# The order of the instruction queues, chosen with another timing model, in a one-core transformer layer

## The chip, the cores and the metric

The kernel runs on one core of a Trainium2 chip. A core has five engines, each with its own queue of instructions, worked off in the order in which it was written at build time: TensorE (PE, with its weight loads, PEld), VectorE (DVE), ScalarE (ACT), GpSimd (POOL) and SyncE (SP), which here mostly starts transfers. Engines wait for each other by semaphores. The metric is the time of one execution on the device, in microseconds.

## The reference

One layer of a latent-diffusion backbone, in float32: 1024 latent tokens and 256 context tokens, width 1024. Cut to what matters:

```
mod   = silu(c) @ w_mod + b_mod                      # shifts, scales, gates of two norms
h, hc = modulated rms_norm of x and of ctx
proj  = h @ w_in                                     # q k v | mLSTM q k v o gates | branch gates
att   = windowed GQA: 16 heads in 4 groups, |i-j| <= 128, all 256 context keys, a sink logit per head
ml    = bidirectional chunkwise mLSTM, started from the context's states, normed, times sigmoid(o)
y     = sigmoid(ga) * (att @ w_branch_att) + sigmoid(gm) * (ml @ w_branch_ml)
x_mid = x + g1 * (y @ w_out)
u     = depthwise conv, width 3, of norm2(x_mid) @ w_up          # 2 x 2816 columns
out   = x_mid + g2 * ((silu(u_g) * u_a) @ w_down)
```

## The kernel before

Every float32 operand is split in a high part (rounded to the fast float32 format of PE) and a low rest: ACT copies the high part, DVE subtracts it (`split_from`, lines 44 and 49). Each product is three matmuls, high by high, high by low and low by high (`mm3`, lines 91 to 93).

The stages follow each other in the source and overlap at their ends. *Start* (to about 105 us): the modulation from sixteen loads `wm` of 512 KB, the norms, transposes of x (`xct`), the context's keys and values. *Attention* (about 105 to 655 us). *mLSTM* (to about 1050 us), with the projections `mo` between its chunk steps. *Branch products and out-projection* (to about 1300 us). *FFN*: 22 units of the up-projection, written as a seven-product scheme on 2x2 blocks (products `pa`, `pb`, `pc`; operand sums and their splits `t1`..`t4`, `b21`, `b22` on DVE and ACT). *Down-projection* in the same scheme (`dx`, `dy`, `finish`), to the end.

The attention's loop takes the 32 pairs (g, b), a group of four heads with one of eight blocks of 128 tokens, as a software pipeline:

```
    for n in range(N + 5):
        if n < N:
            proj(*seq[n])
        if 0 <= n - 1 < N:
            stacks(*seq[n - 1])
        if 0 <= n - 3 < N:
            scores(*seq[n - 3])
        if 0 <= n - 4 < N:
            pv(*seq[n - 4])
        if n not in SKIPS and n < N + len(SKIPS):
            filler(n - sum(s < n for s in SKIPS))
```

`proj` makes q, k and v of one block (24 matmuls into `pq`), with the norm's sums on ACT, DVE and POOL and the rotary products on DVE (lines 520 to 545). `stacks` turns q and k (PE `qt`, then ACT and DVE into `QT`, `KA`, `KB`, lines 553 to 570). `scores` makes for each of four heads the scores `s` (four matmuls, lines 587 to 590) in a PSUM pool with **one** buffer (`s_tile`); DVE adds the mask and takes the row's extreme into `P` (line 593), ACT takes the exponential (line 597), DVE and POOL divide by the sum (lines 601 to 606). `pv` turns `P` (line 625, tile `pt`), splits it (`ph` on ACT, `pl` on DVE) and multiplies with the values (lines 619 and 620, tile `po`); the result `o` leaves by line 636. `filler` is independent work: one half of a 128-column block of the branch gates' projection, 24 matmuls into `g`, 5 to 6 us of PE, whose weights (`fr`) are loaded and split (`fh`, `fl`) just ahead. A `mod_product` (line 212, `macc`) adds one 256 KB slab of the second modulation matrix, loaded into the single buffer `wmb`; lines 221 to 228 (`ms`, `gT`) finish a row of it. The branch weights' sums are lines 1047 to 1050 (`s_ba`).

**What sets the order.** The kernel is written without engine queues of its own. At build time the tile context takes all instructions and picks, in a simulated time, for each engine the next one to be put in its queue: of those whose inputs and buffers are ready in that simulation, the one that stands first in the source. So how long the planner thinks each instruction takes, and when it thinks a buffer comes free, decides which work from further down the source is drawn ahead of work that it believes not yet ready. In ten places `issue_after` holds work back until a named instruction has been put in its queue (for instance lines 309, 445, 909, 1228, 1439 and 1451). The buffers (PSUM: two `mm` for `pq` and `po`, three `tp` for `qt` and `pt`, one `fl` for `g`, the one `s`) turn in the order so found. The chip then keeps each queue's order, whatever its real times are.

## Time and profile before

| | before |
|---|---|
| median of 3 runs | 1943.81 us (1943.13 to 1944.04) |
| profiled execution, span from first to last instruction | 1937.4 us |
| PE busy | 1903.1 us (98%) |
| DVE, ACT, POOL busy | 1442.4, 1000.5, 332.0 us |
| mean granted clock of PE | 0.999 |
| moved by DMA | 298.53 MB, 154 GB/s on average |

The profile is of one execution. A *window* row gives a stretch of it: start and end, its length, the busy time of PE, PEld, DVE, ACT and POOL with their counts of instructions, the granted clock of PE (1.00 is full), and the DMA engines' share and rate. A *group* row gives source line, engine, operation, tile names with shapes and count, then busy time and the mean duration of one in ns, then the time for which the engine was idle just before such an instruction and what ended it. Busy times of neighbours overlap a little, since an engine starts the next instruction before the one in front has quite finished. A *timeline* row gives start and duration in us of one instruction, or of some alike.

### The profile page before, as it was taken

What the parts mean: (1) busy time and instruction counts of PE and PEld (TensorE: products, weight loads), DVE (VectorE), ACT (ScalarE), POOL (GpSimd) and SP (SyncE); (2) the same over time, 40 slices, a digit from 0 to 9 for tenths busy, and PEclk for the clock granted to TensorE, in tenths of its full rate; (3) what the DMA queues carried; (4) which work ended last, traced back from release to release, by engine and by line L of the source; (5) the groups of instructions that cost most, each with busy time, mean ns of one, the idle gap of its engine ahead of it and who ended that gap; (6) DMA issues with size and microseconds to landing.
All of it is one profiled execution on the core that took longest, in us unless ns stands there. A gap on an engine that the chain in (4) does not pass through costs nothing.

```text
span 1937.4 us, 28767 instructions
## 1 busy us (share of the span) xinstructions
PE 1903.1 (98%) x10012; PEld 1631.2 (84%) x10012; DVE 1442.4 (74%) x2886; ACT 1000.5 (52%) x1979; POOL 332.0 (17%) x534
## 2 busy tenths in 40 slices
PE   8999999999999999999999999999999999999999
PEld 3998888888888889999999888788888888888887
DVE  2867878777777666666657878669989898897564
ACT  4845656555556445353536556256545444455441
POOL 1323433433333132131311012010000000000000
PEclk9999999999999999999999999999999999999999
DMA  8731222313222323425235982722354534499841
GB/s 320 231 126 51 80 66 67 95 42 102 60 67 77 125 89 104 144 94 192 88 106 210 376 300 89 279 94 77 141 199 182 195 152 177 160 327 341 307 165 65
DMA packets 139377, 298.53 MB, mean 154 GB/s; under 512 B 15440, under 2 KB 39648, under 8 KB 136416
## 3 DMA queue, kind: packets, MB, share of 16 engines
q1 hardware_dynamic: 124832, 270.48, 40.3%
q10 hardware_dynamic: 14400, 26.22, 4.0%
q8 instruction: 78, 1.28, 0.3%
q14 instruction: 67, 0.55, 0.1%
HBM read 220.55 MB, written 76.10 MB: 153 GB/s over the span
## 4 chain that ended last, share of the span: by engine, by line
PE 83%; DVE 5%; DMA 4%; ACT 4%; issue 2%; POOL 1%; POOLq 0%; ACTq 0%; SPq 0%; DVEq 0%
PE pa L1513 4%; PE pa L1515 4%; PE pa L1514 4%; PE pt L625 3%; PE g L93 3%; PE g L92 3%; PE g L91 3%; PE yb L1515 2%; PE yb L1514 2%; PE yb L1513 2%; PE dx L1515 2%; PE dx L1513 2%; PE dx L1514 2%; PE pb L1513 2%; PE pb L1515 2%
## 5 line engine op out<-in xcount | busy, mean ns | idle before, releaser
L606 POOL TENSOR_SCALAR P<-P,st 128x640 f32<-128x640 f32 (+1 forms) x128 | 115.1, 916 | 261.0 <-DVE st L604 178.3
L597 ACT ACTIVATE P<-P,st 128x640 f32<-128x640 f32 (+1 forms) x128 | 102.6, 801 | 24.6 <-DVE st L593 24.0
L593 DVE CUSTOM_DVE_ANT_0 P<-s,maskA,nsink 128x640 f32<-128x640 f32 (+1 forms) x112 | 103.2, 921 | 9.4 <-PE s L590 7.8
L49 DVE TENSOR_TENSOR pl<-pt,ph 128x512 fp32r<-128x512 f32 x152 | 100.8, 686 | 10.1 <-ACT ph L44 8.6
L44 ACT ACTIVATE ph<-pt 128x512 fp32r<-128x512 f32 x152 | 87.4, 597 | 36.9 <-PE pt L625 32.5
L91 PE MATMUL g<-hH,fh 128*128 128x512 f32 x256 | 102.7, 401 | 0.0
L93 PE MATMUL g<-hH,fl 128*128 128x512 f32 x256 | 100.6, 393 | 0.0
L92 PE MATMUL g<-hL,fh 128*128 128x512 f32 x256 | 100.6, 393 | 0.0
L625 PE MATMUL pt<-ident,P 128*128 128x128 f32 x608 | 92.3, 273 | 3.5 <-POOL P L606 3.1
L91 PE MATMUL pq<-w1h,hH 128*128 128x384 f32 (+1 forms) x256 | 87.1, 340 | 0.2 <-DVE t L545 0.2
L91 PE MATMUL kv<-w1h,hH 128*128 128x384 f32 x256 | 86.5, 339 | 0.8 <-ACT w1h L44 0.8
L93 PE MATMUL pq<-w1h,hL 128*128 128x384 f32 (+1 forms) x256 | 86.7, 339 | 0.0
L92 PE MATMUL kv<-w1l,hH 128*128 128x384 f32 x256 | 86.6, 338 | 0.0
L92 PE MATMUL pq<-w1l,hH 128*128 128x384 f32 (+1 forms) x256 | 86.5, 338 | 0.0
L93 PE MATMUL kv<-w1h,hL 128*128 128x384 f32 x256 | 86.3, 337 | 0.0
L625 PEld LDWEIGHTS pt<-ident,P 128*128 128x128 f32 x608 | 71.1, 140 | 11.5 <-POOL P L606 6.4
L91 PE MATMUL mo<-w1h,hH 128*128 128x256 f32 x256 | 72.6, 284 | 0.4 <-ACT sg L774 0.2
L93 PE MATMUL mo<-w1h,hL 128*128 128x256 f32 x256 | 72.1, 282 | 0.0
L92 PE MATMUL mo<-w1l,hH 128*128 128x256 f32 x256 | 71.9, 281 | 0.0
L1651 ACT ACTIVATE cv<-ua,vecT 128x1024 f32<-128x1024 f32 x22 | 27.4, 1245 | 83.6 <-DVE ua L1624 83.6
L929 POOL TENSOR_SCALAR kwh<-k,gcall 128x128 fp32r<-128x128 f32 x72 | 32.7, 457 | 215.8 <-PE dC L92 112.1
L1513 PE MATMUL dx<-dwh,dfh 128*128 128x512 f32 x176 | 68.7, 390 | 0.0
(587 smaller groups left out, 6392.9 us busy)
## 6 DMA issues: line engine op xcount, KB each, us to landing
ur<-in_w_up SPq DMA_DIRECT2D x22, 1024.0 KB, 4.9
wmb<-in_w_modB SPq DMA_DIRECT2D x48, 256.0 KB, 2.9
f_d<-cv SPq DMA_DIRECT2D x22, 512.0 KB, 2.6
wm<-in_w_modA SPq DMA_DIRECT2D x16, 512.0 KB, 9.2
fr<-in_w_g SPq DMA_DIRECT2D x32, 256.0 KB, 3.1
drf<-fs_d SPq DMA_DIRECT2D x15, 512.0 KB, 6.8
drw<-wt_d SPq DMA_DIRECT2D x14, 512.0 KB, 6.0
w1b<-in_w_cx SPq DMA_DIRECT2D x16, 388.0 KB, 4.0
```

The costliest lines, as they stand in the source:

```text
L44: return nc.scalar.activation(out, in_, AF.Copy, scale=scale)
L49: (nc.vector if eng == "v" else nc.gpsimd).tensor_tensor(lo, src, hi.bitcast(F32), op=ALU.subtract)
L91: nc.tensor.matmul(ps, lh[:, ls], rh[:, rs], start=start and i == 0, stop=False)
L92: nc.tensor.matmul(ps, lh[:, ls], rl[:, rs], start=False, stop=False)
L93: nc.tensor.matmul(ps, ll[:, ls], rh[:, rs], start=False, stop=stop and i == n - 1)
L593: nc.vector.tensor_tensor_reduce(pm[:, :W], ps[:, off : off + W], mask[:, :W], scale=ss[:, h : h + 1], scalar=nsink[:, hh : hh + 1], op0=A ...
L597: nc.scalar.activation(pm[:, :W], pm[:, :W], AF.Exp, bias=st4[:, h : h + 1], scale=-1.0, accum_out=st4[:, 4 + h : 5 + h])
L606: nc.gpsimd.tensor_scalar(Ps[h][:, :W], Ps[h][:, :W], st4[:, 12 + h : 13 + h], 1.0, op0=ALU.mult, op1=ALU.mult)
L625: nc.tensor.transpose(pt[:, h * P : (h + 1) * P], Ps[h][:, kb * P : (kb + 1) * P], ident)
L1513: nc.tensor.matmul(ps, lh, rh, start=start and i == 0, stop=False, skip_group_check=True)
L1514: nc.tensor.matmul(ps, lh, rl, start=False, stop=False, skip_group_check=True)
L1515: nc.tensor.matmul(ps, ll, rh, start=False, stop=stop and i == n - 1, skip_group_check=True)
```

## The change

One argument is added where the tile context is made, in `kernel`, line 1927:

```diff
-    with tile.TileContext(nc) as tc:
+    with tile.TileContext(nc, schedule_with_timeline_sim=True) as tc:
         layer_kernel(tc, A, out)
```

The planner then works with the finer timing model that the language offers instead of its simple one. The operations, their shapes and operands, the pools and the pins are the same. What differs is the order in each engine's queue, and with it which buffer an instance gets and where waits stand: stand-alone waits are 144 instead of 127 on PE, 817 becomes 724 on ACT, 664 becomes 750 on DVE and 589 becomes 560 on SP. ACT has 14 activation table loads instead of 10.

The places where the order differs most:

```
attention      fillers g are put in the queue earlier, up to 12.9 us of them in one block; eleven of the 32
               blocks have none; none is left after the last block's scores. Branch-weight sums s_ba
               (lines 1047 to 1050) stand on DVE before the last scores instead of after them.
mLSTM          the products mo stand in smaller groups between the chunk steps
FFN's start    pa1 and pc1 stand on PE ahead of the transposes x2p1; on DVE t3l, b22l, q2l, t4l stand ahead of t2l
FFN's units    the first products of the next unit (pb t1, pa b11) stand earlier
down-proj.     the last two rows of the modulation (ms, gT, the gate's row) stand some 20 us of PE work later;
               30 matmuls of dy_3 stand in one lump
start          SP: masks, sink, gate bias, first attention weights and first wmb ahead of wm_4 and the later wm;
               POOL: the rotary tables earlier; DVE: seven macc sums earlier
```

## The prediction

> **What bounds the kernel now.** I read the busy shares first, then the slices, then the chain that ended last, and then windows over each stage.
>
> ```profile
> span 1937.4 us, 28767 instructions
> PE 1903.1 (98%) x10012; PEld 1631.2 (84%) x10012; DVE 1442.4 (74%) x2886; ACT 1000.5 (52%) x1979; POOL 332.0 (17%) x534
> ...
> DVE  2867878777777666666657878669989898897564
> ...
> PE 83%; DVE 5%; DMA 4%; ACT 4%; issue 2%; POOL 1%; POOLq 0%; ACTq 0%; SPq 0%; DVEq 0%
> ```
>
> PE is idle for 1937.4 − 1903.1 = 34.3 us in all, so a better order can gain no more than that. The other engines keep up with PE, but DVE only just: nine tenths and more in several late slices. The windows (span, then busy time of PE, its weight loads, DVE, ACT and POOL, then granted clock, DMA share and GB/s) show where the slack is.
>
> ```profile
> 131.80:640.00 508.20, 499.09 (x2836) 437.63 (x2835) 385.36 (x962) 298.56 (x671) 181.36 (x239) 1.00 0.24 70
> ...
> 278.90:291.50 12.60, 12.28 (x74) 10.65 (x73) 11.03 (x28) 7.98 (x19) 2.41 (x4) 1.00 0.14 45
> 378.90:392.60 13.70, 13.13 (x84) 11.92 (x83) 11.41 (x31) 8.08 (x21) 4.99 (x9) 1.00 0.20 64
> ...
> 655.00:1050.00 395.00, 384.31 (x2538) 361.00 (x2536) 263.98 (x754) 181.51 (x458) 93.49 (x214) 1.00 0.37 125
> ...
> 1299.00:1316.00 17.00, 16.46 (x81) 13.36 (x80) 16.45 (x43) 12.93 (x35) 2.47 (x1) 1.00 0.20 62
> 1316.00:1330.00 14.00, 13.73 (x60) 10.83 (x59) 14.00 (x28) 10.37 (x22) 0.00 (x0) 1.00 0.22 76
> 1400.00:1500.00 100.00, 100.00 (x443) 82.81 (x442) 89.21 (x106) 46.94 (x58) 0.00 (x0) 1.00 0.52 192
> ...
> 1760.00:1850.00 90.00, 90.00 (x407) 74.70 (x406) 58.38 (x96) 40.59 (x71) 0.00 (x0) 1.00 0.86 309
> ```
>
> Attention (131.8 to 640) holds 9.1 us of PE's idle time, the mLSTM (655 to 1050) 10.7 us. At the FFN's entry (1299 to 1330) DVE is full too. In the steady FFN PE has no gap at all.
>
> **The change, part by part.** No instruction is dropped, but for four more activation table loads; what moves is the order in each engine's queue. So a cost can only be idle time of PE that the new order forces, and a gain only idle time that it fills. I take the work between two points from the trace of before, start to start, and set it against the new order.
>
> *Attention.* One block is one (g, b) of the 32: scores, softmax, transposes, values, plus projection of a later block. Before, each block also carries one filler, 24 `g` matmuls. The prices:
>
> ```profile
> L593 DVE CUSTOM_DVE_ANT_0 P<-s,maskA,nsink 128x640 f32<-128x640 f32 (+1 forms) x112 | 103.2, 921 | 9.4 <-PE s L590 7.8
> L49 DVE TENSOR_TENSOR pl<-pt,ph 128x512 fp32r<-128x512 f32 x143 | 94.9, 686 | 5.1 <-ACT ph L44 3.6
> L212 DVE SCALAR_TENSOR_TENSOR macc<-wmb,sil,macc 128x512 f32<-128x512 f32 x35 | 29.0, 829 | 21.4 <-DMA wmb<-in_w_modB 21.4
> L567 DVE TENSOR_TENSOR QT<-qt,QT 64x256 fp32r<-64x256 f32 x60 | 25.3, 422 | 6.5 <-ACT QT L44 5.1
> ...
> L636 DVE TENSOR_TENSOR o<-po,o 64x512 f32<-64x512 f32 x30 | 20.4, 681 | 5.9 <-ACT o L44 5.2
> L543 DVE TENSOR_TENSOR qf<-pq,TA 128x256 f32<-128x256 f32 (+1 forms) x58 | 18.3, 316 | 0.0
> L49 DVE TENSOR_TENSOR w1l<-w1r,w1h 128x768 fp32r<-128x768 f32 x17 | 17.4, 1031 | 1.7 <-ACT w1h L44 1.7
> ...
> L593 DVE CUSTOM_DVE_ANT_0 P<-s,mask,nsink 128x512 f32<-128x512 f32 x12 | 9.7, 807 | 1.4 <-PE s L590 1.3
> ```
>
> ```profile
> L1047 DVE TENSOR_TENSOR s_ba<-s_ba,s_ba 128x512 f32<-128x512 f32 x4 | 2.8, 693 | 6.7 <-DMA s_ba<-in_w_ba 6.7
> ```
>
> ```profile
> 308.46 0.42 PE L587 MATMUL s<-KA,QT 128*128 128x384 f32 x1
> ...
> 309.12 1.03 PE L625 MATMUL pt<-ident,P 128*128 128x128 f32 x8
> 309.91 0.48 PE L91 MATMUL g<-hH,fh 128*128 128x512 f32 x1
> ...
> 316.15 0.48 PE L619 MATMUL po<-ph,V 128*128 128x512 f32 x1
> ...
> 317.49 0.40 PE L93 MATMUL g<-hH,fl 128*128 128x512 f32 x1
> ...
> 319.01 0.40 PE L93 MATMUL g<-hH,fl 128*128 128x512 f32 x1
> ...
> 321.31 0.34 PE L91 MATMUL pq<-w1h,hH 128*128 128x384 f32 x1
> ...
> 325.53 0.38 PE L558 MATMUL qt<-ident,qf 128*128 128x128 f32 x2
> ```
>
> ```profile
> 131.80:640.00 508.20, 181.37 (x671) 123.61 (x672) 16.11 (x27) 1.00 0.24 70
> ```
>
> The last row is the same window for tile `g` alone. Start to start, PE needs 0.66 us for a head's scores, 0.79/8 = 0.10 for a `pt` transpose, 1.34/5 = 0.27 for a `po` matmul, 2.30/10 = 0.23 for a `g` matmul (24: 5.5 us) and 4.22 for a projection. The stretch has 112 + 12 = 124 heads on line 593, so 31 blocks: a block is 499.09/31 = 16.1 us of PE against 385.36/31 = 12.4 of DVE. It holds 28 fillers (671 `g` matmuls of 24 each), so a block with one has about 16.6 us of PE work and a block without one 11.1. So PE stays the bound only in a block with its filler. The new order draws fillers ahead: PE's work between the first scores of successive blocks becomes
>
> ```
> block  0    1    2    3    4    5    6    7    8    9   10   11 ... 17   18 ... 25   26   27   28   29   30
> us   17.8 22.6 18.1 14.9 24.6 24.8 17.7 11.9  3.5 17.7  3.9 19.1  10.5  8.2   16.1 11.5 10.5  8.9  6.1  6.7
> ```
>
> and eleven blocks have no `g` matmul left. Scores go through one PSUM buffer (`s_tile`): the scores of head k+1 wait until line 593 has read head k, and DVE does that in its queue's order. So between two heads PE cannot be quicker than DVE's queue. Adding, over disjoint stretches of heads, what DVE's work exceeds PE's: in the old order the sum is 0, in the new one 39 us. The stretches, with heads counted from 0:
>
> ```
> heads     12-15  32-36  37-42  45-51  71-74  76-81  107-110  112-126  smaller
> DVE        11.6    6.0   16.9   20.9    6.5   20.8     6.5     35.9
> PE          8.5    2.9   10.7   18.2    2.4   18.5     3.1     24.2
> excess      3.1    3.0    6.2    2.8    4.1    2.2     3.4     11.7     2.5
> ```
>
> The largest is followed by hand: 14 heads on line 593 at 0.92 (12.9), 15 `pl` at 0.69 (10.3), the branch-weight sums of lines 1047 to 1050, 8 at 0.69 (5.5), which the old order has after 660 us, 3 `o` (2.0), 2 `w1l` (2.1), 4 `QT` (1.7) and 3 to 4 us of small ones: 38 by means, 35.9 start to start, since neighbours overlap a little. PE has 13 heads of scores, 60 `pt` and 34 `po` matmuls there: 8.6 + 6.0 + 34 × 0.27 = 24. This is a bound from below as far as the order goes; it leaves out hand-overs between engines. At the end the last block's softmax has 22 `g` matmuls as cover before and none after: 22 × 0.23 = 5.1 us, from which I take 4. Against it, the new order may fill some of the 9.1 us of gaps; I take 1 for that. Attention: +39 + 4 − 1 = **+42**, from +25 (gaps all filled, overlap of DVE's work better by a tenth) to +65.
>
> The chip's clock adds something.
>
> ```profile
> 930.00:935.00 5.00, 2.91 (x19) 2.25 (x18) 5.00 (x9) 2.69 (x8) 5.00 (x8) 0.92 0.01 3
> 935.00:940.00 5.00, 5.00 (x33) 5.00 (x34) 4.05 (x18) 3.55 (x11) 1.20 (x4) 0.74 0.00 0
> ```
>
> ```profile
> 735.00:740.00 5.00, 3.13 (x25) 2.90 (x24) 4.76 (x15) 3.40 (x12) 5.00 (x9) 1.00 0.00 0
> ...
> 835.00:840.00 5.00, 3.43 (x25) 3.15 (x26) 4.99 (x16) 2.78 (x9) 4.36 (x14) 1.00 0.00 0
> ```
>
> PE busy for 2.91 of 5 us lost clock (0.92, then 0.74: 5 × 0.26 = 1.3 us of work lost); 3.13 and 3.43 of 5 did not. Of the stretches above two fall below that share, 32-36 (2.9 of 6.0) and 71-74 (2.4 of 6.5); most keep PE two thirds busy. **+2**, from 0 to 8 × 1.3 = 10. [...]
>
> *FFN entry.* In the new order `pa1` and `pc1` (5.5 us of PE) stand ahead of the transposes `x2p1`, and DVE has 15 us of work between `acc0<-fb0` and the last `t2l`, where the old order has 7.3 (`t3l`, `b22l`, `q2l` and `t4l` come ahead, 0.34 us each or 0.60, start to start); PE has 10.9 us there, ACT about 1 more in front. The rows of 1299 to 1330 show DVE without a gap, so nothing absorbs it: 15.1 − 10.9 + 0.9 = **+5** (0 to the 7.8 that DVE has more).
>
> *Steady FFN.* A unit is bound by PE (100.00 of 100, DVE 89.21); the new order starts the next unit's first products a little earlier: 0 (−1, to +4 if each of 22 units lost 0.2).
>
> *mLSTM.* Its gaps wait on DVE and POOL (735, 835 and 930); the new order spreads the `mo` products over them: **−3** (−8, most of the 10.7; to +3, one more gap like that at 930: 2.1 and 1.3 of clock).
>
> *Down-projection.* The last rows of `modB` and the gate's transpose come about 20 us later, close to where `finish` must free PSUM, in a window with a DMA share of 0.86, and `dy_3`'s 30 matmuls then stand in one lump: **+2** (0 to 30 × 0.23 = 7).
>
> *Start.* SP issues ten loads (masks, attention weights, the first `wmb`, some 1.95 MB) ahead of the later `wm`; POOL builds the rotary tables earlier.
>
> ```profile
> wm<-in_w_modA SPq DMA_DIRECT2D x16, 512.0 KB, 9.2
> ```
>
> ```profile
> 65.00:70.00 5.00, 2.94 (x20) 2.41 (x20) 4.72 (x6) 4.58 (x10) 5.00 (x6) 1.00 0.55 159
> ```
>
> At `wm`'s pace in the list of DMA issues (0.5 MB in 9.2 us with others beside it, mostly its own kind) 1.95 MB would at most delay a load by several us; `wm` loads are issued well ahead of their products, and PE's 2.1 us without work at 65 may go. **0** (−2 to +6).
>
> *Table loads.* Four more on ACT, which is busy for half the span:
>
> ```profile
> L1011 ACT ACT_TABLE_LOAD x3 | 3.8, 1283 | 0.1
> ```
>
> 4 × 1.28 = 5.1 us, hidden: 0 (to +3, where ACT is late for `ph`). The branch products and the out-projection keep their order: 0.
>
> Sum: 42 + 2 + 5 − 3 + 2 = +48. The profiled execution, 1937.4 us by its span, becomes 1985; the median of 1943.81 stands 6.4 above that span: 1943.81 + 48 = **1992 us**.
>
> **The rivals.** (a) *Faster.* If DVE runs ahead before a stretch without fillers, line 593 is never late, and only filled gaps count. For it: the windows at 278.9 and 378.9 cover blocks with few `g` matmuls, and PE still has 12.28 of 12.6 and 13.13 of 13.7 us. Against it: with one `s` buffer DVE cannot run ahead on scores, and those blocks stand alone. It decides where a block's DVE work fits PE's (11 us against 12, as in those windows). The gain would be the mLSTM's 8, the start's 2 and 5 of attention's 9.1: 1929 us. (b) *Only the end of attention and the FFN entry.* Short stretches are smoothed by neighbours, heads 112 to 126 are not: 12 + 4 + 5 − 3 = +18: 1962. (c) *A chain instead of a sum.* Without cover each block pays its hand-overs, scores to 593 to exponential to POOL to `pt` to `ph` to `po`, and DVE's queue is held by `macc` waiting for `wmb` (21.4 us of waits in the row above, now ahead of heads that PE needs), plus the clock: eleven blocks at 3 us beside the sum, +33: 2025. (d) *No change within what a measurement tells*, 0.2% or 4 us: it needs gain and loss to cancel; 1944.
>
> **How the numbers follow.** My forecast (1975 to 2010) 0.55, (b) 0.15, (c) 0.20, (d) 0.02, (a) 0.08. Range: (a) and (d) with half of the tail of (c) are left out: 1955 to 2030. Faster by over 0.2% 0.07, within 0.2% 0.02, slower 0.91. The three runs of before spread over 0.91 us, so 0.2% is what a measurement tells.
>
> **What would show it.** Right: PE's idle time grows by 40 us or more, nearly all between 200 and 700; idle rows of PE name DVE line 593 (`s` waiting) or `ph` and POOL in the stretches listed; the windows of blocks 7 to 10 and 26 to 31 show DVE near full and PE at two thirds; the FFN's entry shows 5 us more. Wrong: DVE also idle in those windows (a chain, (c)), or PE at 0.98 there (a); clock rows well under 1.00 in attention would make the clock's term bigger; and a longer wait of `pm` for `wm` the start's.

## The result and the profile after

The changed kernel takes 2059.45 us in the median of four runs (2057.10 to 2061.17), the kernel before 1943.47 in four (1941.81 to 1944.04). The ratio is 1.0604, with a 95% interval of 1.0586 to 1.0622: 116 us longer. The forecast was 1992 with a range up to 2030. The direction was right and the size was not; the time lies beyond the range.

The first lines of the profile's page, after:

```profile
span 2055.2 us, 28709 instructions
PE 1942.5 (95%) x10012; PEld 1663.7 (81%) x10012; DVE 1454.2 (71%) x2886; ACT 1004.5 (49%) x1983; POOL 322.4 (16%) x534
...
PE 76%; DVE 9%; DMA 7%; issue 3%; ACT 3%; POOL 1%; ACTq 0%; DVEq 0%; SPq 0%; POOLq 0%
```

PE executes the same 10,012 matmuls. It is idle for 2055.2 − 1942.5 = 112.7 us instead of 34.3 (78 more), and it is busy 39 us longer, because its mean granted clock is 0.976 instead of 0.999. In the chain that ended last, DVE's share has nearly doubled and that of transfers has risen by three points: PE now waits for others, and these wait for data.

The stages, as windows: attention from the first scores to the last `po`, the mLSTM to the last `mt`, and behind the last `op` the FFN's entry, its steady units and the rest to the end. First before, then after:

```profile
131.80:657.60 525.80, 516.65 (x2937) 452.21 (x2936) 395.39 (x983) 308.18 (x693) 185.85 (x252) 1.00 0.24 70
657.60:1050.70 393.10, 382.39 (x2530) 359.64 (x2529) 263.08 (x751) 181.60 (x458) 93.49 (x214) 1.00 0.37 125
...
1298.60:1330.00 31.40, 30.59 (x140) 24.51 (x140) 30.85 (x71) 23.71 (x56) 2.47 (x1) 1.00 0.21 68
1330.00:1721.40 391.40, 391.40 (x1726) 323.61 (x1725) 347.95 (x415) 195.85 (x243) 0.00 (x0) 1.00 0.48 178
1721.40:1937.40 216.00, 211.56 (x942) 175.01 (x940) 142.20 (x225) 82.94 (x145) 0.00 (x0) 1.00 0.65 231
```

```profile
130.80:730.10 599.30, 543.94 (x2954) 472.38 (x2952) 399.12 (x991) 305.71 (x692) 175.08 (x255) 0.97 0.22 68
730.10:1147.90 417.80, 389.96 (x2513) 370.61 (x2512) 270.52 (x744) 191.41 (x468) 93.70 (x211) 0.94 0.33 109
...
1395.00:1426.40 31.40, 26.98 (x113) 21.60 (x112) 27.52 (x68) 19.75 (x49) 3.01 (x1) 0.89 0.20 67
1426.40:1820.10 393.70, 384.09 (x1682) 314.44 (x1682) 332.39 (x395) 189.93 (x234) 0.00 (x0) 1.00 0.45 161
1820.10:2055.20 235.10, 228.24 (x1014) 188.47 (x1012) 161.21 (x253) 93.51 (x163) 0.00 (x0) 1.00 0.66 239
```

Attention lost 599.3 − 525.8 = 73.5 us, the mLSTM 24.7, and the FFN with its down-projection 660.2 − 638.8 = 21.4. The start (131.8 before, 130.8 after) and the branch and out-projections gained 1 us each. In attention PE is idle for 55.4 us instead of 9.1. The entry's window is cut to the same 31.4 us in both, but only 113 matmuls start in it after instead of 140, so the time that they lack appears in the later rows.

What PE waited for, as groups of waits after (us in total, times, longest):

```profile
PE s L587 <- DVE st L593: 27.1, 22, 2.7
PE pt L625 <- POOL P L606: 7.8, 20, 1.1
PE pa L1513 <- ACT ug L44: 6.9, 7, 1.0
PE po L619 <- ACT ph L44: 6.4, 9, 1.6
...
PE pa L1513 <- ACT ua L44: 5.2, 2, 2.7
```

Before, the first of these was `PE s L587 <- DVE st L593: 0.5, 1, 0.5`. So scores wait for line 593, as the forecast named it. But DVE is not simply full. Its own waits after, of which the first two were 9.1 and 8.6 us before, while that for `wmb` was 28.6 and has not grown:

```profile
DVE P L593 <- PE s L590: 67.8, 48, 3.9
...
DVE pl L49 <- ACT ph L44: 50.1, 45, 4.0
...
DVE macc L212 <- DMA wmb<-in_w_modB: 26.8, 20, 2.8
```

PE waits for DVE, and DVE waits for PE, ACT and transfers, in turn. That is the picture of a chain. The end of attention, six blocks without a filler, shows it in windows:

```profile
640.00:665.00 25.00, 19.62 (x106) 17.50 (x105) 18.20 (x49) 14.35 (x33) 11.03 (x16) 0.86 0.06 11
665.00:690.00 25.00, 19.60 (x111) 16.72 (x109) 20.84 (x50) 15.72 (x34) 8.72 (x12) 0.93 0.38 111
690.00:731.00 41.00, 33.67 (x174) 26.52 (x174) 30.13 (x64) 22.95 (x51) 12.89 (x31) 0.92 0.31 95
```

They take 91 us, 15.2 a block. DVE is busy for 69.2 of these, PE for 72.9 even at a clock of 0.86 to 0.93, and no other engine more. No engine is full, and yet a block costs 15 us.

### The profile page after: what moved, and what is told of

Read it like the earlier page. It is cut to its first block, busy times and chain, and to the rows that moved or that the text cites. A ratio compares the mean times of both kernels' runs of the same rounds, so it can differ in the third digit from the quotient of the medians.

```text
span 2055.2 us, 28709 instructions
## 1 busy us (share of the span) xinstructions
PE 1942.5 (95%) x10012; PEld 1663.7 (81%) x10012; DVE 1454.2 (71%) x2886; ACT 1004.5 (49%) x1983; POOL 322.4 (16%) x534
## 4 chain that ended last, share of the span: by engine, by line
PE 76%; DVE 9%; DMA 7%; issue 3%; ACT 3%; POOL 1%; ACTq 0%; DVEq 0%; SPq 0%; POOLq 0%
PE pa L1513 4%; PE pa L1514 4%; PE pa L1515 4%; PE pt L625 2%; PE g L91 2%; PE yb L1514 2%; PE yb L1515 2%; PE g L93 2%; PE g L92 2%; PE yb L1513 2%; DMA wmb<-in_w_modB 2%; PE pb L1514 2%; PE pb L1515 2%; PE pb L1513 2%; PE dx L1513 2%
## 5 line engine op out<-in xcount | busy, mean ns | idle before, releaser
L593 DVE CUSTOM_DVE_ANT_0 P<-s,maskA,nsink 128x640 f32<-128x640 f32 (+1 forms) x112 | 103.0, 920 | 62.4 <-PE s L590 61.3
L49 DVE TENSOR_TENSOR pl<-pt,ph 128x512 fp32r<-128x512 f32 x152 | 100.5, 685 | 50.6 <-ACT ph L44 50.1
L606 POOL TENSOR_SCALAR P<-P,st 128x640 f32<-128x640 f32 (+1 forms) x128 | 101.6, 813 | 214.0 <-DVE st L604 113.4
L44 ACT ACTIVATE ph<-pt 128x512 fp32r<-128x512 f32 x152 | 85.6, 595 | 97.7 <-PE pt L625 97.0
L91 PE MATMUL g<-hH,fh 128*128 128x512 f32 x256 | 104.2, 407 | 6.0 <-ACT fo L44 5.3
L625 PE MATMUL pt<-ident,P 128*128 128x128 f32 x608 | 100.5, 289 | 8.6 <-POOL P L606 7.8
L625 PEld LDWEIGHTS pt<-ident,P 128*128 128x128 f32 x608 | 77.5, 148 | 24.3 <-POOL P L606 13.2
L91 PE MATMUL kv<-w1h,hH 128*128 128x384 f32 x256 | 86.6, 340 | 1.4 <-DVE o L636 1.4
L91 PE MATMUL pq<-w1h,hH 128*128 128x384 f32 (+1 forms) x256 | 87.5, 342 | 0.3 <-DVE o L636 0.2
L91 PE MATMUL mo<-w1h,hH 128*128 128x256 f32 x256 | 76.6, 299 | 1.4 <-ACT sg L774 0.7
L587 PE MATMUL s<-KA,QT 128*128 128x384 f32 (+1 forms) x128 | 49.2, 385 | 27.9 <-DVE st L593 27.1
L44 ACT ACTIVATE dfh<-drf 128x512 fp32r<-128x512 f32 x55 | 34.1, 627 | 74.8 <-PE dy L1514 29.6
L1515 PE MATMUL dx<-dwh,dfl 128*128 128x512 f32 x176 | 68.5, 389 | 0.0
```

The lines of the kernel that those rows point to most:

```text
L44: return nc.scalar.activation(out, in_, AF.Copy, scale=scale)
L49: (nc.vector if eng == "v" else nc.gpsimd).tensor_tensor(lo, src, hi.bitcast(F32), op=ALU.subtract)
L91: nc.tensor.matmul(ps, lh[:, ls], rh[:, rs], start=start and i == 0, stop=False)
L593: nc.vector.tensor_tensor_reduce(pm[:, :W], ps[:, off : off + W], mask[:, :W], scale=ss[:, h : h + 1], scalar=nsink[:, hh : hh + 1], op0=A ...
L606: nc.gpsimd.tensor_scalar(Ps[h][:, :W], Ps[h][:, :W], st4[:, 12 + h : 13 + h], 1.0, op0=ALU.mult, op1=ALU.mult)
L625: nc.tensor.transpose(pt[:, h * P : (h + 1) * P], Ps[h][:, kb * P : (kb + 1) * P], ident)
```

## The experiments

All of them but one set the queues' order by hand. A function added behind the layer ties each instruction to the one that shall stand ahead of it in its engine's queue, from a list of instruction numbers (`ORDER`); the planner is the one of before. With the list of either kernel, that kernel's order comes out. Ratios are to the kernel before on the same chip, with 95% intervals; differences in us are against its median there.

```diff
+def replay(tc, nc):
+    traced = {str(i.name): i for i in nc.cur_bb.bb.instructions}
...
+            if prev is not None:
+                tc.add_manual_dep(
+                    i, prev.name, mybir.DependencyInfo(mybir.DependencyClass.NoSync, mybir.DependencyReason.DATA),
+                    reason="replay",
+                )
+            prev = i
+ORDER = """
...
     with tile.TileContext(nc) as tc:
         layer_kernel(tc, A, out)
+        replay(tc, nc)
```

### Which stage costs what

Three kernels take the changed order in one stage alone, and before's order in the rest. Only the list differs.

*The changed order to the end of attention.*

> Queues in the changed kernel's order until its attention ends (first kv product), in the order of before from there on. If the order of each stage costs its own time, this is before + 70 to 73 us, some 2015 us: 46 us of idle PE and 27 us of slower PE work, all ahead of the first kv product. The rival, that late attention also makes the later stages late (transfers and buffers out of step), gives more than that here, 2030 us and above, with new gaps of PE after the attention.

Measured: 2010.70 us, ratio 1.0356 (1.0331 to 1.0382), 70 us longer.

*The changed order in the mLSTM.*

> Order of before through the attention, the changed order in the mLSTM (from about 660 us of before to the changed kernel's turn of the last head), order of before again from the branch products on. Own cost of the stage: before + 24 us, 1968 us, with the longest gaps where no mo product is left to stand between a state's chain (around the third head's end and ahead of the last mt). The rival, that these gaps were inherited from the attention, gives less than + 8 us.

Measured: 1974.88 us, ratio 1.0175 (1.0153 to 1.0197), 34 us longer. Part of it belongs to the joint of the two orders and to neither of them. This wait of PE is neither among those of before nor among those of the changed kernel:

```profile
PE gTir L822 <- DVE Ic L814: 7.2, 1, 7.2
```

*The changed order from the FFN on.*

> Order of before up to the end of the out-projection (1298 us), the changed order from there on. Own cost: before + 21 us, 1965 us: 3.6 us idle and 3.4 us of half clock at the FFN's entry, the rest in its units and the down-projection (a wait of pa for the copies ua and ug of ACT). The rival, inherited from before the FFN, gives less than + 8 us.

Measured: 1962.54 us, ratio 1.0114 (1.0083 to 1.0146), 22 us longer. The window of its steady part, and PE's waits:

```profile
1330.00:1720.00 390.00, 380.39 (x1665) 311.33 (x1664) 328.87 (x390) 186.38 (x226) 0.00 (x0) 1.00 0.45 161
```

```profile
PE pa L1513 <- ACT ug L44: 6.9, 7, 1.0
PE pa L1513 <- ACT ua L44: 5.2, 2, 2.7
```

What follows: 70 + 34 + 22 = 126 us, or 119 without the joint's 7, against 116 to 118 for the whole. Within the intervals, each stage's loss is its own; none is seen to be handed down from the stage ahead.

### Is it the clock?

The changed order, with matmuls added whose results nobody reads (they go to the filler's PSUM buffer). In the first, 208 of them (24 us of PE, by an estimate from half of the 0.23 us of a `g` matmul, which is twice as wide) stand behind the scores in the blocks without a filler; in the second, 365 (42 us, by the same estimate) stand in 48 of PE's gaps, which measure 52 us together. The places are given by the list.

```diff
+    WARM = {14: 80, 22: 32, 32: 96}
+    def warm(n):
+        if n in WARM:
+            junk = E.fl_tile(f"junk{n}")
+            for _ in range(WARM[n]):
+                nc.tensor.matmul(junk[:, :256], hT[0][0][:, :P], hT[0][0][:, :256], start=True, stop=True)
```

> The changed kernel's whole order, and 208 extra matmuls of 256 columns (0.115 us each, 24 us in all) whose result nobody reads, four behind each head's scores in the thirteen blocks that have no filler left. If idle PE costs clock, and the slower PE then sets the end, PE keeps a clock near 1.00 in those blocks and the time falls by 8 to 20 us although PE has 24 us more to do. If the clock costs nothing because DVE sets the pace in these blocks, the extra work disappears in the gaps: within 5 us. If PE's own work sets the pace, the time rises by up to 24 us.

Measured: 2057.00 us, ratio 1.0606 (1.0575 to 1.0638); attention takes 598 us, against 599 without them:

```profile
131.60:730.00 598.40, 558.73 (x3163) 490.88 (x3161) 398.98 (x991) 304.65 (x692) 174.85 (x255) 0.98 0.23 68
```

```diff
+    WARM = {14: 79, 22: 33, 32: 253}
```

> The changed kernel's whole order, with 365 extra matmuls (256 columns, 0.115 us each, 42 us in all, result read by nobody) put exactly into 48 gaps of PE of 0.3 us and more that its profile shows, in the thirteen blocks without fillers and in the mLSTM, each gap filled to 0.15 us below its length (52 us of gaps). They take no time by themselves. If the idle time also cost clock, and the slower matmuls then cost time, the clock rises to nearly 1.00 there and the time falls by 15 to 30 us. If the clock cost nothing because other engines set the pace, the time stays within 4 us.

Measured: 2053.87 us, ratio 1.0583 (1.0565 to 1.0601), with these windows of attention and mLSTM:

```profile
132.70:733.10 600.40, 564.58 (x3175) 490.86 (x3174) 398.74 (x991) 305.49 (x692) 174.29 (x255) 0.99 0.23 68
733.10:1148.30 415.20, 394.40 (x2659) 374.83 (x2657) 269.63 (x744) 191.76 (x468) 98.07 (x211) 0.98 0.33 109
```

The clock rose from 0.97 and 0.94 to 0.99 and 0.98, 42 us of work came on top, and the two stages together took 1016 us, against 1017 without it. So the lower clock looks for the most part like a consequence: PE runs slowly where it would otherwise wait. The two ratios differ by 0.0021, 4 us, and by their intervals by some 9 at the most. That is the net of a faster clock and more work, so it bounds the clock's price only as far as the added work hid in gaps.

### Which of the moved instructions?

*Before's order, with the `g` matmuls alone at their changed places on PE.* Their loads and splits are left free.

> The order of before in every queue, with the fillers' matmuls g alone put in the changed kernel's places on PE (their loads, splits and copies go where they are ready). Going score by score through PE's and DVE's queues, with one score buffer and 0 to 0.2 us for a hand-over, the waits add to 16 to 21 us, in the changed order itself to 39 to 47, where the attention in fact lost 73. By that ratio this costs 20 to 35 us, 1965 to 1980 us. If the drawn-ahead fillers are the whole of the attention's loss, 2010 us. If DVE's order is the whole of it, less than + 8.

Measured: 2045.56 us, ratio 1.0545 (1.0528 to 1.0562), 106 us longer, where 20 to 35 were expected. This is too much to be the fillers' places alone: with loads and splits placed anew, their weights come late.

```profile
PE g L91 <- ACT fh L44: 16.8, 3, 6.3
PE s L587 <- DVE st L593: 15.2, 18, 1.5
```

It shows that moving fillers can cost that much, and not how much of the change it was.

*The opposite: the changed planner, with each filler's matmuls held behind the scores of its turn.*

```diff
+            E.sc = nc.tensor.matmul(ps[:, 512 : 512 + NCTX], q, KcB[:, g], start=False, stop=True)
...
+        with ExitStack() as pin:
+            if E.sc is not None:
+                pin.enter_context(tc.issue_after(E.sc.ins))
+            mm3(nc, ps, FW[c], hT, sl(0, P), sl(t * 512, 512))
```

> The changed kernel's planner, with each filler's matmuls held on PE behind the scores of its own turn of the loop, so that every block but three has its 24 again. If the fillers are the whole of the attention's loss, some 1990 us. The waits by PE's and DVE's queues still add to 27 to 38 us here (before: 0; changed: 39 to 47), since DVE's queue keeps macc sums in lumps ahead of line 593; by the same ratio as above the attention loses 45 to 60 us instead of 73, and the whole takes 2030 to 2047 us, if the later stages come out as in the changed kernel.

Measured: 2051.70 us, ratio 1.0577 (1.0560 to 1.0595); attention took 600 us, no less. PE's waits for line 593 are 23.1 us and those for POOL 13.8 (7.8 in the changed kernel). The fillers' lumps are thus not the only thing wrong, or the planner, held back there, put something else in the way.

*Before's order, with the `mo` products alone at their changed places.*

> The order of before in every queue, with the matmuls mo of the mLSTM alone in the changed kernel's places on PE (their copies go where they are ready). If drawing mo ahead, away from the states' chains and from the last head's end, is what costs the mLSTM its 24 to 34 us, this costs 15 us or more, 1958 us and above, with an idle stretch of about 5 us ahead of the last mt. If it is the other engines' order there, less than + 8 us.

Measured: 1997.96 us, ratio 1.0297 (1.0282 to 1.0312), 58 us longer, more than twice what the mLSTM lost. Here too the free instructions spoil the answer: `PE kv L91 <- ACT w1h L44: 24.0, 3, 8.7` is a wait that the changed kernel doesn't have. Nothing is concluded from it.

### Loads ahead of the chain

*The changed order, in which the 48 `macc` sums read a table that lies in SBUF, instead of the slab just loaded.* The slabs are loaded all the same.

```diff
     w = pool.tile([P, 512], F32, tag="wmod", name=f"wmb{n}", bufs=1)
     nc.sync.dma_start(w, E.A["w_modB"][n // KT][:, n % KT])
+    w = E.resident
...
+    E.resident = TA[0].rearrange("p b c -> p (b c)")
```

> The changed kernel's whole order; the 48 macc sums of the attention read a rotary table that lies in SBUF instead of the slab wmb, so no macc waits for a load (the loads still run; the modulation's values are not the reference's). In the changed kernel DVE stands idle 26.6 us in front of macc during the attention and the chain of work passes through these loads for 39 us of it. If scores stuck behind a macc that waits for its load make up the loss beyond the 39 to 47 us of the queues' own work, the attention falls by 20 to 39 us, to 2020 to 2040 us in all. If others are in the way anyhow, less than 8 us.

Measured: 2046.96 us, ratio 1.0539 (1.0517 to 1.0562), about 12.6 us less than the changed kernel by the ratios. Its profile shows 8 us less in attention (591 us), at the edge between the two expectations. The waits are plain to see on the chain that ended last in the changed kernel (start, length, what):

```profile
186.03 2.68 DMA wmb<-in_w_modB
188.74 0.75 DVE macc L212
...
197.51 2.75 DMA wmb<-in_w_modB
200.35 0.76 DVE macc L212
201.13 2.67 DMA wmb<-in_w_modB
```

These sums stand in DVE's queue ahead of the next line 593 and wait for a load of 2.7 us that starts only when the sum before it has left the one buffer (200.35 + 0.76 = 201.11). But they are a part of the loss, not the bulk of it. Nor has this wait grown much: DVE stands idle ahead of `macc` for 26.8 us in this attention, and for 21.4 in that of before, where PE had the fillers to do.

*The changed order without the branch sums* (lines 1047 to 1050 and 1055 to 1058, their loads and their stores); the branch products read the plain weights in their place. And the same with before's order, to compare.

```diff
     def branch_sums():
         n, i = SUMS.pop(0)
+        return
...
-        sums = lambda s, i: lambda k0: s[:, i, k0 : k0 + 2]
+        sums = lambda s, i: lambda k0: s[i // 2][:, i % 2 * 4 + k0 : i % 2 * 4 + k0 + 2]
...
-    sd = E.sums_d
+    sd = dict(t_at=A["w_ba"], s_ba=A["w_ba"], s_bm=A["w_bm"])
```

> The changed kernel's whole order with the twelve groups of branch sums left out (their loads, 48 DVE operations and stores; the branch products read the plain weights in their place, so the output is not the reference's). If the sums, which stand among the next head's state updates on DVE here and wait there for transfers, and hold the buffers that the copies of mo need, make the mLSTM's loss, some 24 us go there and 5 to 10 at the attention's end: 2020 to 2032 us. If the place of the mo products makes it, less than 10 us go.

> The same left out under the order of before: the yardstick for the run without sums. The mLSTM has 10.7 us of idle PE there, so at most that goes; by the waits seen on PE, which name other work than the sums, 0 to 4 us: 1936 to 1943 us.

Measured: 2033.63 us with the changed order, ratio 1.0473 (1.0449 to 1.0498), 25 us less than the changed kernel; 1940.51 with before's, ratio 0.9993 (0.9981 to 1.0004), no change. The mLSTM, 417.8 us in the changed kernel, takes

```profile
728.40:1123.90 395.50, 378.36 (x2512) 358.85 (x2512) 245.29 (x704) 191.22 (x468) 93.01 (x211) 0.98 0.20 62
```

395.5 us, 22 less, where before the change it took 393.1. So the sums cost nothing that shows where before's order has them, between two heads of the mLSTM, and nearly all of the mLSTM's loss where the new order has them, among the state updates (`C`, `CL`, `nm`, `kwl`) of the next head. At the attention's end, where 5 to 10 us were expected of them, they cost 3: the attention takes 596.4 us instead of 599.4.

DVE does not wait longer for their transfers: it is idle ahead of the lines of the sums for 24 us in the changed kernel and for 27 in the one before. What changed is what stands behind them in the queue. The chain of the changed kernel shows one such place: a sum waits for its load, `ql` stands behind the sum, and PE, which needs `ql`, is idle for 2.8 us (`PE S L91 <- DVE ql L49: 2.8, 1, 2.8`).

```profile
970.05 4.22 DMA t_at<-attT_d
974.30 0.70 DVE t_at L1056
975.07 0.57 issue
975.64 0.68 DVE ql L49
```

ACT's queue is held too, since the loads of the sums are issued from it. The sums' buffers are two, so a new load waits until the store of the sums ahead has left them. Here is that store in the chain, and then what ACT did, with its idle time in brackets:

```profile
991.92 6.14 DMA t_at_d<-t_at
```

```profile
998.14 0.82 ACTq L1046 DMA_DIRECT2D s_bm<-in_w_bm  x2
999.06 0.48 ACT L980 ACTIVATE nm<-i,gcall 128x257 f32<-128x257 f32 x1 [2.97 <-DMA t_at_d<-t_at]
```

PE's next product `i` comes after a wait of 2.7 us for this `nm` (`PE i L91 <- ACT nm L980: 3.7, 3, 2.7`). How the 22 us divide between the two queues wasn't measured. Not every gap nearby is the sums': here is a stretch in which PE does little, first in the changed kernel and then in the run without the sums, where it stands as well.

```profile
1005.00:1010.00 5.00, 1.94 (x7) 1.52 (x7) 5.00 (x12) 3.46 (x13) 3.11 (x4) 0.58 0.14 54
```

```profile
985.00:990.00 5.00, 2.04 (x9) 1.64 (x9) 5.00 (x16) 4.00 (x14) 3.99 (x6) 0.88 0.00 0
```

### How much cover did the fillers give?

*Before's order with the fillers cut* from 24 matmuls to 3, in each of 32; 672 are left out, at 0.23 us some 155 us of PE; attention has 696 `g` matmuls from its first scores to its last `po`, so 696 × 7/8 × 0.23 = 140 us there. The rest of the order stays.

```diff
-        mm3(nc, ps, FW[c], hT, sl(0, P), sl(t * 512, 512))
+        mm3(nc, ps, FW[c][:1], hT, sl(0, P), sl(t * 512, 512))
```

> The order of before with each filler cut from 24 matmuls to 3 (the other 672 left out, so the branch gates are not the reference's). PE's work falls by 672 x 0.23 = 155 us, 136 us of it in the attention after the first scores, from 16.1 to 11.7 us a block; DVE has 12.4 us a block. If PE's and DVE's queues can work side by side without loss, a block takes 12.4 us and the time falls by 115 to 135 us. If the hand-overs from engine to engine set the pace of a block without fillers (the changed kernel's take 13 to 15 us where their PE work is 6 to 11), a block takes 13.5 to 15 us and the time falls by 55 to 95 us.

Measured: 1921.63 us, ratio 0.9898 (0.9870 to 0.9926): 21 us less for 155 us of work, far below both expectations. This is the run that overturned the forecast's model. Its attention:

```profile
132.60:644.40 511.80, 433.05 (x2326) 368.43 (x2326) 391.07 (x984) 307.79 (x692) 186.54 (x252) 0.91 0.25 72
```

```profile
PE s L587 <- DVE st L593: 30.9, 29, 3.8
PE pt L625 <- POOL P L606: 26.8, 46, 2.6
PE po L619 <- ACT ph L44: 13.6, 12, 2.8
```

511.8 us instead of 525.8, with DVE busy for 391, ACT for 308, and PE for 433 at a clock of 0.91. No engine is full, and PE waits for each link of the softmax in turn. So in this order a second bound, the chain of hand-overs with the loads that hold DVE's queue, lies only 14 us below PE's 98%.

*The changed order with the fillers cut in the same way.*

> The changed kernel's whole order, each filler cut from 24 matmuls to 3 as before (672 matmuls, 155 us of PE work, left out; the branch gates are not the reference's). Under the order of before that took 20.6 us off, since a block without filler work takes 16 us too: the fillers had run in time that was there. If the changed order's loss in the attention is that its lumped fillers no longer run in such time, it loses most of them as cost: the attention falls by 65 to 95 us, the whole to 1965 to 1995 us. If the loss lies in the other queues' order (macc, sums, hand-overs), the fall is 20 to 40 us as under the order of before, 2020 us and above.

Measured: 2000.43 us, ratio 1.0303 (1.0289 to 1.0317), 58 us less than the changed kernel and between the two expectations:

```profile
123.20:673.90 550.70, 441.27 (x2346) 380.48 (x2344) 399.16 (x991) 304.06 (x692) 176.28 (x255) 0.89 0.25 74
```

Its attention is 599.3 − 550.7 = 48.6 us shorter than the changed kernel's, where before's order gave 14.0. So, if the parts simply add, the fillers' places cost 48.6 − 14.0 = 35 us, and the rest of the new order, on all queues, 550.7 − 511.8 = 39 us. (The other 8 us or so of the 58 are the start, whose end came at 123.2.) Together that is the 73.5. In the 39 lie 24.5 us more of waiting for line 593 (`PE s L587 <- DVE st L593: 55.4, 33, 6.2`). They also hold some of the fillers still, since the three matmuls left of each stand at the changed places: these wait for the copy `fo` of the filler ahead (`PE g L91 <- ACT fo L44: 8.2, 7, 5.2`), for 0.9 us under before's order.

*Before's order with the fillers cut and the `macc` sums reading the table.* This is both edits above.

> The order of before, fillers cut to 3 matmuls and macc reading the resident table, so that no load holds DVE's queue. If loads at the head of DVE's queue set the 16 us a block of the run with cut fillers, a block takes 12.5 to 14 us and the time falls by 65 us and more below that run, under 1860 us. If the hand-overs between PE, DVE, ACT and POOL set them, it falls by less than 30 us.

Measured: 1894.40 us, ratio 0.9753 (0.9737 to 0.9770), 28 us less than with the loads, by the ratios. Its attention, and PE's first two waits (in this kernel the lines of the softmax stand two further down):

```profile
126.00:607.80 481.80, 416.73 (x2327) 353.82 (x2327) 389.22 (x984) 307.16 (x693) 189.34 (x252) 0.95 0.26 77
```

```profile
PE pt L627 <- POOL P L608: 29.4, 48, 2.6
PE s L589 <- DVE st L595: 23.3, 25, 2.0
```

Attention takes 481.8 us, 30 less than with the loads. A block still needs 481.8 / 32 = 15.1 us with DVE busy for 12.2 of it. So the loads make up 0.9 us a block of the second bound, and the 2.9 us by which a block exceeds DVE's work are left to the hand-overs.

### The FFN's steady units

*The changed order from the FFN on, with the copy `ug` moved ahead of the split of `r2h` on ACT in 18 units.* Only the list differs, in ACT's queue.

> Order of before up to the FFN and the changed order from there on, as in the run with the changed FFN alone, but on ACT the copy of ug stands ahead of the split r2h again in the 18 units where the changed order has it behind. If that split, which first waits for PE, holds the copy and so the PSUM bank that the next unit's first product needs, the seven gaps of 1.0 us at pa go: 5 to 9 us less than the 22 us of that run, 1.0070 to 1.0085 of before. If the gaps come from DVE's or PE's order, no change: 1.011.

Measured: 1962.81 us, ratio 1.0110 (1.0094 to 1.0125), against 1.0114 (1.0083 to 1.0146) without the swap. PE's waits for `ug` shrank from 6.9 us to

```profile
PE pa L1513 <- ACT ug L44: 4.8, 7, 0.7
```

2 us less, which the intervals can't tell from nothing; 5 to 9 were expected if the split of `r2h` were the cause. Why ACT brings `ug` and `ua` late stays open.

## Why the prediction was wrong in size

*Attention: +42 forecast, +73.5 measured.* The place and the first wait were right: 36 of the 55.4 us of PE's idle time lie in the blocks without fillers, and most of its waits for line 593 too. The idle time of the whole stage grew by 46 us (of 78 in all, where the prediction looked for nearly all of it here); the other 27 of the 73.5 are PE busy for longer, at a clock of 0.97. The step that failed is the price of a block. It took the larger of PE's and DVE's work, 11.1 and 12.4 us where there is no filler. From first scores to first scores in the trace, thirteen blocks have no `g` matmul (the prediction counted eleven), and they took 15.1 us on average; a block takes 511.8 / 32 = 16.0 us in before's order when the fillers are cut everywhere. The eleven blocks with 39 to 54 `g` matmuls took 22.7 us, where a block of before took 525.8 / 32 = 16.4. So a filler that moved cost most of its 5.5 us where it went, since that block was full, and gave little back where it left. That is rival (c), a chain instead of a sum, and what the prediction named as its sign came: DVE is idle too in blocks 26 to 31, busy for 69.2 of 91 us. I gave it 0.20. That its sum for this stage, 42 + 33 = 75, comes so near is luck in part: of the 42, the largest stretch has 5.5 us of `s_ba` and 11.7 of excess, and without the sums the attention is 3 us shorter. The windows at 278.9 and 378.9, read as PE bound with few fillers, did not show it; each is a short stretch between neighbours with fillers, which a chain can draw on, but that reason wasn't tested.

The working by stretches of heads also put all of the loss on the fillers' absence and on `s_ba` at the end. The runs put 35 us on the fillers' places and 39 on the rest of the order (that this equals the forecast's 39 is chance). Of the 73.5, the waits of `macc` are 8 and the sums 3, each left out alone with the fillers in place. How much of the 39 is theirs without that cover wasn't measured (in before's order without fillers `macc`'s loads are worth 30), and the rest of it stays open.

*mLSTM: −3 forecast, +24.7 measured.* The step looked at the `mo` products alone and put the branch sums, which move too and bring loads, stores and two buffers with them, at nothing here; the forecast counted such sums only at the end of attention. They are 22 of the 24.7. Rival (c) had the mechanism, a DVE queue held by an instruction that waits for a transfer, and I had applied it only to `macc`.

*FFN entry: +5 forecast.* Right in mechanism: the window of the entry holds 26.98 us of PE in 31.4 at a clock of 0.89 (0.50 from 1412 to 1418). Against 30.59 before, 3.6 us more are idle and by estimate 0.11 × 31.4 = 3.5 are lost to the clock, 7 in all, within the range of 0 to 7.8.

*Steady FFN: 0 forecast, to +4.* PE's idle time between 1426.4 and 1820.1 is 393.70 − 384.09 = 9.6 us, where it had none. DVE's 89.21 of 100 had looked like slack for a reordering; the waits are for the copies `ug` and `ua` of ACT instead, which is busy for half of the time. A busy share of a half does not say that each copy comes in time.

*Down-projection: +2.* The one wait of PE in this window, 2.4 us at 1836, is of `pa` for `ua`: a product of the last up-projection units, which now stand among the first `dx`. So the size is right by luck, and neither the late gate nor the lump of `dy_3` shows.

*Clock: +2.* The working took a cost for idle time of PE alone, with this term beside it. But PE is busy for 39 us more with the same matmuls. Three stretches of its table, not two, lie below the share that it named (107-110 as well, with 3.1 of 6.5), and in the trace there are stretches such as these:

```profile
325.00:330.00 5.00, 1.39 (x5) 1.04 (x4) 4.94 (x17) 2.38 (x8) 2.37 (x4) 0.66 0.38 106
...
485.00:490.00 5.00, 5.00 (x22) 4.90 (x22) 1.53 (x3) 2.77 (x7) 1.71 (x3) 0.50 0.00 0
```

The second shows half clock (0.50) with PE busy throughout, after 5 us in which it was busy for 1.43: a head's four scores take 1.22 us start to start there, instead of 0.66. The forecast allowed up to 10 us for eight stretches, at the 1.3 us that the rows at 930 had given for one, and the 39 us are more than that. But 42 us of work put into the gaps raised the clock from 0.976 to 0.990 and changed the time by less than the two intervals can tell, so the term on the path was small, as forecast, while the slowness was not.

*Start 0, table loads 0, branch products 0:* the start and the branch products came out 1 us shorter each; no wait of PE behind a table load shows among its groups.

With the measured terms for mLSTM (+28), FFN (+14) and the start and branch products (−2) in place of the forecast's, rival (c) would have given 2025 + 28 + 14 − 2 = 2065, near the 2059 found. That says no more than that its attention was near.

## What to carry to other kernels

An engine busy for 98% of a stage is one bound; ask what the stage would take if that engine's spare work were gone, because a chain of hand-overs may lie right below it (here 14 us below, for 140 us of work), and then independent work is free only as long as it is spread evenly (the same work left out of the changed order made attention 48.6 us shorter). In a queue that keeps its order, an instruction fed by a transfer belongs where nothing that others need stands behind it, and so does the issue of its load: the same twelve groups of sums cost nothing at one place and 25 us at another, though DVE waited for their transfers for 27 us at the first and 24 at the second. When pricing a reordering, list every group of instructions that moves past a dependent chain, with its loads and buffers, and price a block by the measured time of a block without its cover, not by the largest busy time in it.

## What was not expected of the hardware

Extra matmuls were free here. With 42 us of them in the gaps, the granted clock rose from 0.976 to 0.990 over the span and the time did not rise (ratio 1.0583, against 1.0604 without them, with intervals that overlap). And PE can be called busy for all of a 5 us window at half clock (0.50 at 485), so its busy share understates the idleness of a stage that waits: in the run with the fillers cut, PE's busy time in attention fell by 84 us, though about 140 us of work had gone.
